# Moving the first feed-forward gate into its norm, reordering the feed-forward pools, and starting the last stage's weights before its norm

## The chip, the cores and the metric

The kernel runs on one core of a Trainium2 chip. The core has five engines, each with its own instruction queue that it works off strictly in order: TensorE (PE, matrix products; its weight loads are shown as PEld), VectorE (DVE), ScalarE (ACT), GpSimd (POOL) and SyncE (SP), which here only issues DMA transfers. The engines wait for each other by semaphores. The metric is the device time of one execution in microseconds (us).

## The reference

Two layers work on 256 context and 256 latent tokens of width 1024. All data are float32.

```python
for layer in range(2):
    # six modulation vectors for each of the two segments, from the conditioning vector
    sh1, sc1, g1, sh2, sc2, g2 = split(silu(c) @ mod_w[layer] + mod_b[layer], 6)
    h = rmsnorm(x, norm_mix_g) * (1 + sc1) + sh1
    x = x + g1 * mixer(h)              # layer 0: GLA and mLSTM heads; layer 1: SSD scan
    h = rmsnorm(x, norm_ffn_g) * (1 + sc2) + sh2
    u = depthwise_conv(h @ w_up)       # 1024 -> 2 * 2816
    x = x + g2 * ((silu(u_g) * u_a) @ w_down)
return rmsnorm(x_latent, final_norm_g) # layer 1 only needs the latent tokens after its mixer
```

## The kernel before

Activations are kept transposed: eight tiles `xT[k]` of 128 channels by 512 tokens. A float32 product is made of three matrix products of rounded parts (`mm3`, L186 to L188): high weights by high activations (`wh`, `hh`), low weights by high activations (`wl`, `hh`), high weights by low activations (`wh`, `hl`). Weights come through a `Stream`: a 1 MB load into a `raw` tile (L159; the very first one in two halves, L159 and L167), whose two halves ("units" of eight 128x128 blocks) are split by `split`: ACT writes `wh` (L174), then POOL or DVE writes `wl` (L175). The streams of the feed-forward up projections give all of L175 to POOL. A stream starts its next load as soon as one of its two `raw` buffers is free.

`Norm` gathers squares on ACT (L294), sums them over channels with matrix products against ones (`colsum`, L132), takes a reciprocal root in a row of short DVE steps (`rsqrt`, L112 to L123), and spreads the result over partitions (`spread`, L140, copied by ACT, L141). `norm_mod` then makes, for each of eight k: a DVE product (L323), ACT's `hh` (L329) and DVE's `hl` (L331). Layer 0 does this for two segments, so 16 steps of each kind; layer 1's last stage for one, so 8.

The modulation vectors come in chunks, twelve a layer. A chunk loads 2 MB of `modw` (L241, tiles `rawm`), runs eight 32-row matrix products (L249; the trace counts each twice), and `mod_out` copies the result by ACT (L269), transposes it on PE (L272) and reduces it on DVE (L276, L277). Chunks 10 and 11 of a layer are the feed-forward gate, g2. Most chunks of layer 1 are "fills": a stream calls one of them with each of its loads.

Three places matter here.

**Place one** is the end of layer 0's mixer, from 290 us to 355 us. The program there writes four head ends (`finish`: DVE and ACT steps, and transposes L739), with layer 0's chunks 10 and 11 among them, loaded into the mixer's buffers `b4`. Then the out-projection follows, 192 matrix products of 128x512.

**Place two** is layer 0's feed-forward norm and the first up product behind it, from 355 us. PE fills the norm with chunk (1,2). The first product works on four output tiles at once, k by k, which makes 96 matrix products of 128x512.

**Place three** is the last stage, from 1010 us: the end of layer 1's out-projection (`odd_out`), whose weights `wout` come by DMA; its norm; and the first up product (`project(0)`, 48 matrix products of 128x256). Between `odd_out`'s fourth and fifth output tile the program loads both gate chunks of layer 1, 4 MB. After `project(0)`, PE works through 22 rounds of up and down products, and POOL splits the weights for nearly all of them.

The order of instructions on each engine is the program's order, but for what the scheduler of the language moves by priorities. A buffer pool opened later may lie on memory that an earlier pool has just given up; its first writes then wait for the last readers of what lay there.

## Time and profile before

| what | value |
|---|---|
| runs | 1277.53, 1278.04, 1280.91 us (median 1278.04) |
| the profiled execution's own time | 1280.36 us |
| its span (first to last instruction) | 1278.6 us |
| PE busy | 1227.3 us, 96% of the span, at a mean granted clock of 0.989 |
| DVE busy | 928.4 us, 73% |
| ACT busy | 593.9 us, 46% |
| POOL busy | 424.4 us, 33% |
| DMA | 191.45 MB, 150 GB/s on average |

PE is busy nearly throughout, so the time is the work of PE, plus the places where PE waits, plus what it loses where its clock is at half. All three places of the change are among those.

### The profile page before, as it was taken

How to read it: one execution, taken by the hardware profiler on the slowest of the kernel's cores; microseconds unless marked ns; L12 is line 12 of the kernel's file. 1: busy time of each engine (PE TensorE's matmuls, PEld its weight loads, DVE VectorE, ACT ScalarE, POOL GpSimd, SP SyncE). 2: the span in 40 equal slices, each digit the busy share in tenths (PEclk: the TensorE clock that was granted, in tenths of full speed). 3: DMA queues.
4: the chain of work that ended last, by engine and by line, in shares of the span. 5: the costliest groups of instructions: out<-in, count | busy, mean ns of one | idle time of the engine just before them, and what ended most of it. 6: DMA issues, size and time to landing. Idle time of an engine off the chain costs nothing. (4 is left out here: it accounts for less than half of the span.)

```text
span 1278.6 us, 18743 instructions
## 1 busy us (share of the span) xinstructions
PE 1227.3 (96%) x7094; PEld 1001.2 (78%) x7094; DVE 928.4 (73%) x2064; ACT 593.9 (46%) x937; POOL 424.4 (33%) x246
## 2 busy tenths in 40 slices
PE   7989999999999999999999999999999998999996
PEld 5557787876867767888888897888887886999994
DVE  5483889487567776227776478888888955999997
ACT  4463345344344443214443246665656554655552
POOL 0100000000125555326666000022222314899992
PEclk9989999999999999999999999999999998999998
DMA  9556202334436565232211224453544394455431
GB/s 372 211 178 231 105 27 72 136 107 165 165 110 269 220 232 191 74 129 99 99 66 59 90 92 122 163 157 118 175 130 136 99 345 150 165 197 175 178 114 64
DMA packets 40107, 191.45 MB, mean 150 GB/s; under 512 B 4609, under 2 KB 10569, under 8 KB 21073
## 3 DMA queue, kind: packets, MB, share of 16 engines
q1 hardware_dynamic: 36512, 185.48, 41.6%
q10 hardware_dynamic: 3504, 4.77, 1.2%
q8 instruction: 56, 0.92, 0.3%
q14 instruction: 35, 0.28, 0.1%
HBM read 189.03 MB, written 1.20 MB: 149 GB/s over the span
## 5 line engine op out<-in xcount | busy, mean ns | idle before, releaser
L175 POOL TENSOR_TENSOR wl<-raw,wh 128x1024 fp32r<-128x1024 f32 x120 | 289.3, 2418 | 494.3 <-ACT wh L174 492.3
L174 ACT ACTIVATE wh<-raw 128x1024 fp32r<-128x1024 f32 x226 | 237.1, 1054 | 154.3 <-PE gps L188 98.2
L186 PE MATMUL gps<-hh,wh 128*128 128x512 f32 (+1 forms) x824 | 291.1, 354 | 6.9 <-ACT hh L329 4.9
L187 PE MATMUL gps<-hh,wl 128*128 128x512 f32 (+1 forms) x824 | 290.0, 352 | 1.1 <-DVE wl L175 1.1
L188 PE MATMUL gps<-hl,wh 128*128 128x512 f32 (+1 forms) x824 | 290.1, 353 | 0.0
L800 DVE SCALAR_TENSOR_TENSOR y<-mps,fcw,y 128x255 f32<-128x255 f32 (+3 forms) x592 | 245.5, 432 | 47.0 <-ACT y L794 33.5
L186 PEld LDWEIGHTS gps<-hh,wh 128*128 128x128 f32 x824 | 155.7, 189 | 42.9 <-issue 12.5
L175 DVE TENSOR_TENSOR wl<-raw,wh 128x1024 fp32r<-128x1024 f32 x106 | 129.8, 1234 | 78.0 <-ACT wh L174 77.9
L188 PE MATMUL mps<-hl,wh 128*128 128x256 f32 (+1 forms) x544 | 174.8, 322 | 1.4 <-DVE hl L331 1.4
L186 PE MATMUL mps<-hh,wh 128*128 128x256 f32 (+1 forms) x544 | 175.6, 323 | 0.3 <-ACT hh L329 0.3
L187 PE MATMUL mps<-hh,wl 128*128 128x256 f32 (+1 forms) x544 | 175.0, 322 | 0.0
L187 PEld LDWEIGHTS gps<-hh,wl 128*128 128x128 f32 x824 | 156.1, 189 | 24.0 <-issue 3.2
L188 PEld LDWEIGHTS gps<-hl,wh 128*128 128x128 f32 x824 | 156.1, 190 | 20.9 <-issue 1.7
L186 PEld LDWEIGHTS mps<-hh,wh 128*128 128x128 f32 x544 | 103.7, 191 | 15.5 <-issue 7.0
L188 PEld LDWEIGHTS mps<-hl,wh 128*128 128x128 f32 x544 | 103.5, 190 | 9.1 <-DVE hl L331 1.6
L187 PEld LDWEIGHTS mps<-hh,wl 128*128 128x128 f32 x544 | 103.6, 190 | 7.8
L800 DVE SCALAR_TENSOR_TENSOR y<-gps,fcw,y 128x189 f32<-128x189 f32 (+3 forms) x180 | 77.5, 438 | 22.0 <-ACT y L794 18.2
L794 ACT ACTIVATE y<-mps,fcw 128x256 f32<-128x256 f32 (+1 forms) x68 | 41.1, 638 | 89.0 <-PE mps L188 89.0
L186 PE MATMUL gps<-mh,wh 128*128 128x512 f32 (+1 forms) x198 | 73.5, 371 | 0.0
L188 PE MATMUL gps<-ml,wh 128*128 128x512 f32 (+1 forms) x198 | 73.5, 371 | 0.0
L187 PE MATMUL gps<-mh,wl 128*128 128x512 f32 (+1 forms) x198 | 73.4, 371 | 0.0
L342 DVE SCALAR_TENSOR_TENSOR x<-gps,mod,x 128x256 f32<-128x256 f32 x56 | 24.2, 478 | 45.1 <-PE gps L188 45.1
(293 smaller groups left out, 1899.5 us busy)
## 6 DMA issues: line engine op xcount, KB each, us to landing
raw<-in_up SPq DMA_DIRECT2D x42, 1024.0 KB, 4.9
rawm<-in_modw SPq DMA_DIRECT2D x36, 1024.0 KB, 6.7
raw<-in_win SPq DMA_DIRECT2D x32, 1024.0 KB, 5.3
raw<-in_dn SPq DMA_DIRECT2D x20, 1024.0 KB, 5.6
raw<-in_wout SPq DMA_DIRECT2D x10, 1024.0 KB, 6.2
rawm<-in_mods SPq DMA_DIRECT2D x8, 1024.0 KB, 14.2
R<-crd SPq DMA_DIRECT2D x32, 256.0 KB, 4.2
rawm<-in_modw SPq DMA_DIRECT2D x8, 512.0 KB, 6.3
```

Of the source, the lines that this page charges most:

```text
L174: s.activation(out=hi[:, :n], in_=rw, func=AF.Copy)
L175: self.eng(u).tensor_tensor(out=lo[:, :n], in0=rw, in1=hi[:, :n].bitcast(F32), op=ALU.subtract)
L186: te.matmul(out=ps, lhsT=lhi, rhs=rhi, start=first, stop=False)
L187: te.matmul(out=ps, lhsT=llo, rhs=rhi, start=False, stop=False)
L188: te.matmul(out=ps, lhsT=lhi, rhs=rlo, start=False, stop=last)
L342: v.scalar_tensor_tensor(out=xT[m][:, a:b], in0=ps[:, a - base:b - base], scalar=gt[:, m, ci:ci + 1], in1=xT[m][:, a:b], op0=ALU.mult, op1 ...
L794: self.E.s.activation(out=y, in_=ps, func=AF.Identity, scale=self.fcw[:, c + 4:c + 5], bias=self.fcw[:, c + 9:c + 10])
L800: self.E.v.scalar_tensor_tensor(out=o, in0=i, scalar=self.fcw[:, ti * 10 + wi:ti * 10 + wi + 1], in1=o, op0=ALU.mult, op1=ALU.add)
```

## The change

First, layer 0's chunks 10 and 11 no longer stand among the head ends. Their loads are issued after the last `finish`, chunk 10 into `b4`, chunk 11 into the mixer's `tok` buffers. Their matrix products are written after the out-projection, so they lie in the norm; chunk 11's `mod_out` is called after `norm_mod` (`rest()`). Chunk (1,2), which lay in the norm, becomes the first of the fills.

Second, the feed-forward's pools are opened in another order: `fw` (a table of convolution weights) and `ur` first, then `fp` and `fs`. `ur` holds the raw weights of the up projection in both layers; in the last stage the down projection, which used `ur` before, uses the general pool.

Third, in the last stage `early` splits the first two up units and loads only chunk (1,10) between output tiles; chunk (1,11) is loaded behind `odd_out`. Chunk (1,10)'s matrix products lie in the norm now. `issue_after` holds back, in the scheduler's order, chunk 10's output until the last step of `rsqrt`, and chunk 11's output and the convolution's first steps until the last `hh` of the norm.

```diff
     with ExitStack() as st:
-        even_mixer(E, st, acts, pss0, nrm.add)
+        rest = even_mixer(E, st, acts, pss0, nrm.add)
...
     r = nrm.row()
-    mod_chunk(1, 2, rawp, mps)
     acts = norm_mod(0, 3, 4, SEGS, r)
+    rest()
...
-    E.mod_chunk(0, 10, sp, E.vps, "b4", 4, 4)
     finish(0)
     finish(1)
     finish(2)
-    E.mod_chunk(0, 11, sp, E.vps, "b4", 4, 4)
     finish(3)
+
+    mods = [list(E.mod_load(0, 10, sp, "b4", 4, 4)), []]
+    for i in range(2):
+        raw = T_([P, 4, 516], "tok", bufs=2).rearrange("p a b -> p (a b)")[:, :2048]
+        nc.sync.dma_start(out=raw, in_=A["modw"][0, 11, :, i * 2048:(i + 1) * 2048])
+        mods[1].append(raw)
...
+    E.mod_go(0, 10, mods[0], E.gps)()
+    return E.mod_go(0, 11, mods[1], E.gps)
...
+        fw, self.ur = st.enter_context(E.tc.tile_pool(name="fw", bufs=1)), st.enter_context(E.tc.tile_pool(name="ur", bufs=2))
+        self.fcw = fw.tile([P, NFC], F32, tag="fcw", name=E.nm("fcw"))
+        E.nc.scalar.dma_start(out=self.fcw, in_=E.A["fcw"][l])
         self.fp = st.enter_context(E.tc.tile_pool(name="fp", bufs=1))
         self.fs = st.enter_context(E.tc.tile_pool(name="fs", bufs=6))
...
-    up = E.Stream(A["up1"], 44 * KD, ahead=2, eng=lambda u: g)
-    dn = E.Stream(A["dn1"], FF * KD, pool=ur, eng=lambda u: g if u < FF - 2 else v, parts=lambda u: dw if u < FF - LAG else E.wp)
+    up = E.Stream(A["up1"], 44 * KD, ahead=2, pool=ur, eng=lambda u: g, parts=lambda u: dw if u < 2 else E.wp)
+    dn = E.Stream(A["dn1"], FF * KD, eng=lambda u: g if u < FF - 2 else v, parts=lambda u: dw if u < FF - LAG else E.wp)
...
-    odd_out(E, gated, nrm.add, lambda: mods.extend((list(E.mod_load(1, 10, ur)), list(E.mod_load(1, 11, mw)))))
+
+    def early():
+        up.split(0)
+        up.split(1)
+        mods.append(list(E.mod_load(1, 10, mw)))
+
+    odd_out(E, gated, nrm.add, early)
+    mods.append(list(E.mod_load(1, 11)))
+
     turn(0)
     turn(4)
-    E.mod_go(1, 10, mods[0], mps)
     r = nrm.row()
-    E.mod_go(1, 11, mods[1], mps)
+    gate10 = E.mod_go(1, 10, mods[0], mps)
+    with tc.issue_after(E.last["rsqrt"]):
+        gate10()
+    gate11 = E.mod_go(1, 11, mods[1], mps)
     acts = E.norm_mod(1, 3, 4, SEGS[1:], r)
+    normed = E.last["norm"]
+    with tc.issue_after(normed):
+        gate11()
```

On PE, at place two (the norm between the out-projection and the first up product), this stood before; `rawm` is chunk (1,2):

```order
L132 MATMUL vps_3008<-ones,acc 128x128 x4
L249 MATMUL mps_3042<-rawm_3043,spad 32x512
L132 MATMUL vps_3008<-ones,t_558_3006 128x128 x4
L249 MATMUL mps_3042<-rawm_3043,spad 32x512 x3
L249 MATMUL mps_3042<-rawm_3049,spad 32x512 x4
L272 MATMUL mps_3057<-c_104,t_569_3055 128x128 x3
L140 MATMUL vps_3036<-c_104,ry_3024 128x128 x4
L272 MATMUL mps_3057<-c_104,t_569_3055 128x128
L186 MATMUL gps_3148<-hh_3068,wh_3154 128x512
L187 MATMUL gps_3148<-hh_3068,wl_3155 128x512
```

and this stands now (line numbers are 2 higher); `gps_2980` is chunk 10, `tok` chunk 11, `vps_3223` chunk (1,2):

```order
L134 MATMUL vps_2968<-ones,acc 128x128 x4
L251 MATMUL gps_2980<-rawm_2678,spad 32x512
L134 MATMUL vps_2968<-ones,t_550_2966 128x128 x4
...
L251 MATMUL gps_2980<-rawm_2684,spad 32x512 x2
L274 MATMUL gps_2991<-c_104,t_554_2989 128x128 x4
L251 MATMUL gps_2998<-tok_2686,spad 32x512 x4
L251 MATMUL gps_2998<-tok_2688,spad 32x512 x4
L142 MATMUL vps_3023<-c_104,ry_3011 128x128 x4
L251 MATMUL vps_3223<-rawm_3224,spad 32x512 x4
L251 MATMUL vps_3223<-rawm_3230,spad 32x512 x4
L188 MATMUL mps_3125<-hh_3032,wh_3130 128x512
```

Chunk 10 takes the place that chunk (1,2) had, chunk 11 stands ahead of the spread (L140, now L142), and chunk (1,2) behind it. The transposes of chunks 11 and (1,2) stand in the middle of the first up product. The first load of the up projection is written to memory where the `tok` buffers lie, so it waits for PE's products from `tok`.

On ACT, at place three (from the last square of the norm to the first convolution steps), this stood before; `t_1611` is chunk 10, `t_1619` chunk 11:

```order
L174 ACTIVATE wh_9690<-raw_9660 128x1024
L294 ACTIVATE t_1603_9507<-x_95 128x256
L908 COPY xt<-mps_9529 128x512
L908 COPY xt<-mps_9535 128x512
L269 COPY t_1611_9550<-mps_9541 128x512
L141 COPY rstd_9559<-vps_9573 128x256
L269 COPY t_1619_9586<-mps_9577 128x512
L141 COPY gate<-vps_10862 128x512
L329 ACTIVATE hh_9597<-t_1621_9595,mod_3_115 128x256
```

and this stands now; `t_1619` is chunk 10, `t_1646` chunk 11:

```order
L296 ACTIVATE t_1604_9517<-x_95 128x256
L917 COPY xt<-mps_9543 128x512
L917 COPY xt<-mps_9549 128x512
L271 COPY t_1619_9582<-mps_9573 128x512
L143 COPY rstd_9555<-vps_9569 128x256
L331 ACTIVATE hh_9602<-t_1622_9600,mod_3_115 128x256
...
L331 ACTIVATE hh_9644<-t_1643_9642,mod_3_115 128x256
L271 COPY t_1646_9648<-mps_9591 128x512
L176 ACTIVATE wh_9665<-raw_9663 128x1024
```

Two weight splits that stood just ahead of the last square, and the two copies between `rstd` and the first `hh`, are gone from there; chunk 11's copy comes after all eight `hh`. On PE, chunk 11's transposes still stand ahead of `project(0)`'s first product:

```order
L142 MATMUL vps_9569<-c_104,ry_9557 128x128 x2
L274 MATMUL mps_9584<-c_104,t_1619_9582 128x128 x4
L251 MATMUL mps_9591<-rawm_9527,spad 32x512 x4
L251 MATMUL mps_9591<-rawm_9529,spad 32x512 x4
L142 MATMUL vps_10865<-c_104,mod_5_117 128x128 x4
L274 MATMUL mps_9650<-c_104,t_1646_9648 128x128 x4
L188 MATMUL mps_9661<-hh_9602,wh_9261 128x256
```

Both chunks' products now lie in this norm, where before only chunk 11's did.

## Rows read from the trace of the kernel before

**Rows 1.** The page: busy time, share of the span and instructions of each engine.

```profile
PE 1227.3 (96%) x7094; PEld 1001.2 (78%) x7094; DVE 928.4 (73%) x2064; ACT 593.9 (46%) x937; POOL 424.4 (33%) x246
```

**Rows 2.** Timeline of PE, 295 to 316 us: start, length, what, idle time before.

```profile
300.69 1.05 PE L249 MATMUL vps<-rawm,spad 128*32 128x512 f32 x4
304.43 1.05 PE L249 MATMUL vps<-rawm,spad 128*32 128x512 f32 x4 [2.69 <-DMA rawm<-in_modw]
305.41 0.50 PE L188 MATMUL gps<-hl,wh 128*128 128x512 f32 x1
...
307.67 1.06 PE L249 MATMUL vps<-rawm,spad 128*32 128x512 f32 x8
308.67 0.50 PE L186 MATMUL gps<-hh,wh 128*128 128x512 f32 x1
...
314.78 0.60 PE L272 MATMUL vps<-c,t 128*128 128x128 f32 x4
315.13 0.48 PE L186 MATMUL gps<-hh,wh 128*128 128x512 f32 x1
```

**Rows 3.** Timeline of PE, 354 to 375 us.

```profile
355.14 1.05 PE L132 MATMUL vps<-ones,acc 128*128 128x128 f32 x8
...
358.19 1.92 PE L249 MATMUL mps<-rawm,spad 128*32 128x512 f32 x14
...
361.24 0.60 PE L140 MATMUL vps<-c,ry 128*128 128x128 f32 x4
...
363.97 0.60 PE L186 MATMUL gps<-hh,wh 128*128 128x512 f32 x1 [2.02 <-ACT hh L329]
```

**Rows 4.** Windows: length, busy PE, PEld, DVE, ACT, POOL, clock, DMA share, GB/s.

```profile
362.00:364.00 2.00, 0.03 (x1) 0.03 (x1) 1.93 (x7) 1.45 (x4) 0.00 (x0) 1.00 1.03 430
364.00:366.00 2.00, 2.00 (x5) 1.61 (x6) 2.00 (x6) 1.04 (x3) 0.00 (x0) 0.55 1.00 422
366.00:368.00 2.00, 2.00 (x7) 1.57 (x6) 2.00 (x6) 1.31 (x3) 0.00 (x0) 0.59 0.94 397
1030.00:1042.00 12.00, 11.41 (x98) 10.68 (x97) 5.19 (x11) 2.97 (x7) 0.00 (x0) 1.00 1.02 423
```

**Rows 5.** Timeline of SP, 285 to 400 us: the first load of the up projection.

```profile
322.54 0.33 SPq L159 DMA_DIRECT2D raw<-in_up  x1
```

**Rows 6.** The page: two groups of instructions, and one kind of DMA issue.

```profile
L175 POOL TENSOR_TENSOR wl<-raw,wh 128x1024 fp32r<-128x1024 f32 x120 | 289.3, 2418 | 494.3 <-ACT wh L174 492.3
L174 ACT ACTIVATE wh<-raw 128x1024 fp32r<-128x1024 f32 x226 | 237.1, 1054 | 154.3 <-PE gps L188 98.2
...
raw<-in_up SPq DMA_DIRECT2D x42, 1024.0 KB, 4.9
```

**Rows 7.** Timelines of DVE and of POOL, 336 to 376 us.

```profile
369.63 0.47 DVE L331 SCALAR_TENSOR_TENSOR hl<-t,mod,hh 128x256 fp32r<-128x256 f32 x1
...
372.86 3.13 DVE L331 SCALAR_TENSOR_TENSOR hl<-t,mod,hh 128x256 fp32r<-128x256 f32 x3 [1.57 <-ACT hh L329]
...
372.51 2.41 POOL L175 TENSOR_TENSOR wl<-raw,wh 128x1024 fp32r<-128x1024 f32 x1 [13.62 <-ACT wh L174]
```

**Rows 8.** The chain that ended last, 1000 to 1110 us.

```profile
1029.19 13.30 DMA raw<-in_wout
...
1063.62 1.04 ACT wh L174
...
1066.21 2.28 DVE rw L113
```

**Rows 9.** Timelines of PE, then of POOL, 1030 to 1085 us.

```profile
1062.18 0.61 PE L132 MATMUL vps<-ones,acc 128*128 128x128 f32 x4
...
1076.03 0.39 PE L186 MATMUL mps<-hh,wh 128*128 128x256 f32 x1 [0.30 <-ACT hh L329]
...
1083.47 0.39 PE L188 MATMUL mps<-hl,wh 128*128 128x256 f32 x1 [1.42 <-DVE hl L331]
...
1063.79 4.66 POOL L175 TENSOR_TENSOR wl<-raw,wh 128x1024 fp32r<-128x1024 f32 x2 [3.47 <-ACT wh L174]
```

More of the change, by code (lines that the diff above doesn't have):

```diff
@@ L106, in block_kernel @@
     g.memset(ones, 1.0)
+    last = {}
     def rsqrt(ss, scale, eps):
@@ L122, in rsqrt @@
         v.scalar_tensor_tensor(out=w, in0=w, scalar=-0.5, in1=m, op0=ALU.mult, op1=ALU.mult)
-        v.scalar_tensor_tensor(out=y, in0=w, scalar=1.5, in1=y, op0=ALU.add, op1=ALU.mult)
+        last["rsqrt"] = v.scalar_tensor_tensor(out=y, in0=w, scalar=1.5, in1=y, op0=ALU.add, op1=ALU.mult).ins
         return y
@@ L250, in mod_go @@
                 k += 1
-        mod_out(l, 4 * j, 4, ps, psa)
+        return lambda: mod_out(l, 4 * j, 4, ps, psa)
     def mod_chunk(l, j, pool=rawp, psa=vps, tag="raw", n=2, bufs=None):
-        mod_go(l, j, mod_load(l, j, pool, tag, n, bufs), psa)
+        mod_go(l, j, mod_load(l, j, pool, tag, n, bufs), psa)()
     def mod_part(q, pool, psa):
@@ L328, in norm_mod @@
             for ci, a, b in segs:
-                s.activation(out=h_[:, a:b], in_=y[:, a:b], func=AF.Identity, bias=sh[:, k, ci:ci + 1])
+                last["norm"] = s.activation(out=h_[:, a:b], in_=y[:, a:b], func=AF.Identity, bias=sh[:, k, ci:ci + 1]).ins
             for ci, a, b in segs:
@@ L386, in block_kernel @@
     fill0 = [lambda j=j: mod_chunk(0, j) for j in (4, 5, 8, 9, 6, 7)]
-    fill1 = [lambda j=j: mod_chunk(1, j) for j in (3, 0, 1, 4, 5, 8, 9, 6, 7)]
+    fill1 = [lambda j=j: mod_chunk(1, j) for j in (2, 3, 0, 1, 4, 5, 8, 9, 6, 7)]
     E.fill0, E.W0 = fill0, W0
@@ L785, in __init__ @@
         self.E, self.n, self.lo = E, n, n - TL
+        fw, self.ur = st.enter_context(E.tc.tile_pool(name="fw", bufs=1)), st.enter_context(E.tc.tile_pool(name="ur", bufs=2))
+        self.fcw = fw.tile([P, NFC], F32, tag="fcw", name=E.nm("fcw"))
+        E.nc.scalar.dma_start(out=self.fcw, in_=E.A["fcw"][l])
         self.fp = st.enter_context(E.tc.tile_pool(name="fp", bufs=1))
         self.fs = st.enter_context(E.tc.tile_pool(name="fs", bufs=6))
-        self.fcw = self.fp.tile([P, NFC], F32, tag="fcw", name=E.nm("fcw"))
-        E.nc.scalar.dma_start(out=self.fcw, in_=E.A["fcw"][l])
     def centre(self, ps, ti):
@@ L793, in centre @@
         c = ti * 10
-        self.E.s.activation(out=y, in_=ps, func=AF.Identity, scale=self.fcw[:, c + 4:c + 5], bias=self.fcw[:, c + 9:c + 10])
+        self.last = self.E.s.activation(out=y, in_=ps, func=AF.Identity, scale=self.fcw[:, c + 4:c + 5], bias=self.fcw[:, c + 9:c + 10]).ins
         return y, ps, ti
@@ L831, in conv_ffn @@
     cv = Conv(E, st, 0, T)
-    ur = st.enter_context(E.tc.tile_pool(name="ur", bufs=2))
-    up = E.Stream(E.A["up0"], 44 * KD, fill, 1, 2, pool=ur, eng=lambda u: g)
+    up = E.Stream(E.A["up0"], 44 * KD, fill, 1, 2, pool=cv.ur, eng=lambda u: g)
     first = []
@@ L890, in last_ffn @@
     cv = Conv(E, st, 1, TL)
-    ur, dw, mw = (st.enter_context(tc.tile_pool(name=n, bufs=2)) for n in ("ur", "dw", "mw"))
+    ur = cv.ur
+    dw, mw = (st.enter_context(tc.tile_pool(name=n, bufs=2)) for n in ("dw", "mw"))
     lp = st.enter_context(tc.tile_pool(name="lp", bufs=1))
     LAG = 4
-    up = E.Stream(A["up1"], 44 * KD, ahead=2, eng=lambda u: g)
-    dn = E.Stream(A["dn1"], FF * KD, pool=ur, eng=lambda u: g if u < FF - 2 else v, parts=lambda u: dw if u < FF - LAG else E.wp)
+    up = E.Stream(A["up1"], 44 * KD, ahead=2, pool=ur, eng=lambda u: g, parts=lambda u: dw if u < 2 else E.wp)
+    dn = E.Stream(A["dn1"], FF * KD, eng=lambda u: g if u < FF - 2 else v, parts=lambda u: dw if u < FF - LAG else E.wp)
     fng = lp.tile([P, D], F32, tag="fng", name="fngr")
@@ L935, in project @@
             pa = E.gemm_f(up, 16 * j + 8, KD, acts, 256, T, lambda: both[:, TL:])
-        return cv.centre(pg, FF + j), cv.centre(pa, j)
+        r = cv.centre(pg, FF + j), cv.centre(pa, j)
+        centred[:] = [cv.last]
+        return r
     hm = []
@@ L953, in last_ffn @@
     part = lambda: None
-    nxt = project(0)
+    with tc.issue_after(normed):
+        nxt = project(0)
     for j in range(FF):
@@ L961, in last_ffn @@
         if j in more:
-            more[j]()
+            with tc.issue_after(centred[0]):
+                more[j]()
         h, part = cv.tile(cg, ca, v, part, "", LAG + 2, v if j == FF - 1 else g)
```

1 line of the change is left out of this document (added).

## The prediction

> **What bounds the kernel now.** I read first the page's busy times: PE is busy in 96% of the span [rows 1], so time is won or lost only where PE waits or where its clock is at half. The list of PE's waits and the timelines of the engines at the three places then show where that is. Place one: PE waits 2.69 us for a chunk of modulation weights, with the chunk's matrix products around it [rows 2]. Place two: from the norm's first sum at 355.14 to the first up product at 363.97 lie 8.8 us, of which PE spends the last 2.02 waiting for `hh` [rows 3]; after it the granted clock is 0.55 and 0.59 in two windows of 2 us, between the levels 1.2 and 2.4 GHz, which costs 2 x 0.45 + 2 x 0.41 = 1.7 us [rows 4]. Place three: the chain that ended last runs through a `wout` load of 13.30 us [rows 8], while DMA moves 423 GB/s [rows 4], about as much as in any window I saw; then through a weight split and a DVE step of 2.28 us [rows 8]; from the first sum at 1062.18 to the last wait of `project(0)` at 1083.47 [rows 9], and to its end some 0.5 us later, it is 21.8 us.
>
> **Place one, gain 9.4 us.** The products and the transposes of chunks 10 and 11 leave. From 300.69 to 305.41 that is 4.7 us with the wait in it; 1.0 us from 307.67 to 308.67, and there are four such rows in all, at 296.80, 307.67, 310.49 and 312.33: 4.0 us; the transposes take 0.35 (314.78 to 315.13), twice: 0.7 [rows 2]. Sum 9.4. What stood in line around them on ACT (two copies) and DVE goes too, so I let no new wait of PE for the head ends come up; if the 2.69 us also covered that chain, up to 2.7 us of the gain is gone. So the out-projection ends, and the norm's sum begins, at 345.8 instead of 355.1.
>
> **Place two, loss 10.4 us.** Chunk 10 takes the place of chunk (1,2), same shape, same time. Chunk 11's 1.92 [rows 3] goes ahead of the spread, which moves from 6.1 to about 8.2 us behind the sum: 2.0 lost. Chunk (1,2) fills the wait for `hh` and costs nothing there. The `hh` would let the up product start at 345.8 + 8.8 + 2.0 = 356.6.
>
> But the weights are late. Before, the first up load was issued at 322.54 [rows 5], 41 us ahead. Now it writes where `tok` lay and waits for chunk 11's products, so for 353.9. A 1 MB load lands 4.9 us after its issue [rows 6]; half of it is less by 0.5 MB at 430 GB/s [rows 4], so I estimate 3.7 (bounds 3 and 4.9). Then ACT takes 1.05 and POOL 2.42 [rows 6]: 353.9 + 3.7 + 1.1 + 2.4 = 361.1 for the first low products, 4.5 behind `hh`. This is 2.9 earlier than 363.97. The clock's 1.7 us stays, since PE again stands idle before; the transposes of chunks 11 and (1,2) now lie inside the product: 0.7.
>
> Then there is the company that POOL's splits now have. Before, the four splits of the first product were done by 359, before DVE's norm steps began. Now they run beside them. An `hl` step takes 0.47 us alone, so three take some 1.2; three of them took 3.13 where a POOL split of 2.41 ran from 372.51 [rows 7]: about 1.9 lost to one split. ACT's order makes a chain of it: the second, third and fourth `wh` stand behind the `hh` steps of the next k, which wait for DVE, which waits for POOL's split before. A link is 2.4 (split) + some 1.3 (three or four DVE steps) + 1.1 (`wh`), 4.8 us. So the weights of k = 2 come at 365.9, of k = 4 at 370.7. PE now runs two output tiles through k = 0 to 5 first: 36 products at 0.2265, 8.2 us, and 1.7 for the clock would end at 371.0; chained, the last DVE step for k = 5 ends some 2 us after 370.7, and PE at about 374.1. So 3.2 lost (bounds: 0, if DVE's steps slip in between, and 9.7, four whole splits). Net of places one and two: 2.9 - 0.7 - 3.2 = **1.0 us slower**.
>
> The Trainium skill, page "SBUF — State Buffer", section "Who interferes with whom", says that a VectorE instruction with two SBUF inputs contends with a GpSimd instruction that reads SBUF, and that the one which comes second blocks wholly; the row of 3.13 us agrees. By it alone the four splits could cost DVE 9.7 us, and with my other terms the two places would lose 7.5.
>
> **Place three, gain 4.0 us.** Ahead of the `wout` load that ends the wait of 13.30 stand 4 MB of chunks; now 3 MB (two chunk loads, two halves and one whole of up weights). With DMA at 423 GB/s [rows 4] 1 MB is 2.4 us, so I let `odd_out` end 2.4 earlier (bounds 0, if the load is held by a buffer, and 3.6, if the 16 products of chunk 10, which leave here, count too). In the norm, the last square no longer stands behind the split at 1063.62 and the one before it: 1.7 us; the reciprocal root no longer stands beside POOL's splits from 1063.79 [rows 9], so its step takes 0.17 as its neighbours do instead of 2.28 [rows 8]: 2.1. But `project(0)` does not start early. Its first product stands behind chunk 11's transposes, whose copy on ACT now comes after all eight `hh`. From the sum at 1062.18: square and second sum 1.7, root 2.4, spread and copy 1.0, 16 DVE steps of 0.4 with the last `hh` 0.8 before their end, so `hh` at 1073.5; copy 0.6, transposes 0.6, so the first product at 1074.7 instead of 1076.03 [rows 9]; 48 products of 0.119, 5.7, and again 1.8 for the clock after 4.8 us of idleness: 1082.2 instead of 1083.9. So 1.7, not 3.8. Sum with 2.4: 4.1, say **4.0 us faster**.
>
> All else counts as nothing: the table of convolution weights waits on ACT's queue for chunk 11 too, but ahead of the spread's copy, which is later anyway; ten fills instead of nine move the same products; the reordered pools give no new wait that I find behind the first load. In the last stage POOL has four splits (9.7 us) more to do after the norm than before. Behind the copy at 1074.1 ACT makes `wh`, and the third up unit's split ends at 1077.6; six more at 2.42 (two of them for the down product) and the seventh unit's ends at 1092.1. PE wants it four units of 24 x 0.119 = 2.85 behind 1082.2, at 1093.6: 1.5 us to spare.
>
> **The sum.** 1.0 slower and 4.0 faster: 3.0 us. Against the profiled execution's own 1280.36 this is 1277.4; that execution was 2.3 above the median, so against 1278.04 it is **1275.0 us**. This measurement can tell about 0.3%, 3.8 us, from no change; 3.0 lies inside.
>
> **The rivals.**
> *The splits and DVE don't hurt, or only little.* For it: DVE has gaps of a step's length while POOL waits for ACT. Against it: the row of 3.13 us. Then places one and two gain 2.2, and with an earlier landing 3; total 6.2 to 7: 1271.5. Chance 0.22.
> *The weights aren't late at all,* because the load gets its memory or the product starts on its high parts. Then the first product starts at 356.6, without the clock's loss perhaps: 9.4 - 2.0 - 0.7 + 4.0 = 10.7: 1267.3. The order of reads and writes speaks against it. Chance 0.08.
> *`wout` lands no earlier,* since the new up loads cost as much or a buffer holds it: 0.6 gained, 1277.4, also no change that can be told. Chance 0.2.
> *Slower: POOL's splits in the norm block DVE one by one.* If each of the four costs PE its whole 2.42 us, the loss S is 9.7 instead of 3.2, and the total is 6.2 - S = -3.5; it tells as slower from S = 10.0, or from 7.6 if `wout` also stays where it was. What speaks for it is the same row, what speaks against it is that PE needs a new pair of weights only every 2.7 us and has slack at low clock. 1282.0. Chance 0.13. The page named above, read strictly, leads here.
>
> **How the numbers follow.** The forecast has 0.37, `wout` unmoved 0.2, both within 0.3%; with some of their tails outside, same 0.5. Faster is 0.22 + 0.08 and a tail of 0.06: 0.36. Slower is 0.13 and a small tail: 0.14. From 1270 (quick weights and no stalls, wholly) to 1281.5 (just short of the slower rival) no more than 2 in 10 is left out; the forecast's own range is 1273 to 1278.
>
> **What would show it.** Right: no wait of PE for `rawm` near 300 us; the norm's sum at about 346; the first up load issued at about 354 and the first low product at about 361; `hl` steps of 2 to 3 us beside POOL's splits; a wait for the third pair of weights; in the last stage the first norm sum near 1060 on the old clock, a root without a step of 2 us, a wait of some 5 us for ACT's copy of chunk 11 ahead of `project(0)`, and no wait of PE for `wl` behind it. Wrong: a first up load before 350; the norm sum later than 348; PE waiting for POOL's `wl` after 1085.

## The result, and the profile after

The changed kernel takes **1287.59 us** (median of 4 runs, 1285.82 to 1289.32), the kernel before beside it 1278.15 (4 runs): a ratio of 1.0065, with a 95% interval of 1.0043 to 1.0088. It is slower by 5.5 to 11.2 us; 1275.0 was forecast, with 1281.5 as the upper end. The profiled execution after has an own time of 1285.82 us, a span of 1284.0 and a mean granted clock of 0.986.

The page, busy time of each engine; [rows 1] before:

```profile
PE 1224.8 (95%) x7094; PEld 1003.9 (78%) x7094; DVE 925.2 (72%) x2064; ACT 594.0 (46%) x937; POOL 428.9 (33%) x246
```

PE is busy with as many instructions for 2.5 us less, and the span is 5.4 longer: the time that was added is mostly waits. Read between marks that the timelines of both have, the two kernels compare like this (us):

| stretch | before | after | difference |
|---|---|---|---|
| start to the first sum of place two's norm | 355.14 | 345.58 | -9.56 |
| that sum to the start of the 96th up product | 34.65 | 47.59 | +12.94 |
| to the first norm sum of layer 1 | 354.53 | 359.26 | +4.73 |
| to the end of layer 1's scan | 272.97 | 273.20 | +0.23 |
| to the first sum of place three's norm | 44.89 | 42.46 | -2.43 |
| to PE's last product | 204.60 | 204.21 | -0.39 |

They add up to +5.5, as the two executions differ (1285.82 - 1280.36). The medians differ by 9.4. Part of that is the stretch ahead of place two, which varies by some 3 us between executions: the sum stood at 355.1, 356.0 and 355.8 in three kernels with the old mixer's end, and at 345.6, 348.4, 348.7, 348.7 and 348.3 in five with the changed one (this profile and experiments 3, 4, 6 and 8). The gain ahead of place two is 9.6 in this pair and about 7.5 by the middle values.

Part of it is lost before place one. The first half of chunk 11 is loaded into `tok` long before the last `finish`, here at 244.73 (SP's timeline). It runs beside small loads of the mixer, and DVE waits for one of them (DVE's timeline):

```profile
244.73 0.33 SPq L773 DMA_DIRECT2D tok<-in_modw  x1
```

```profile
252.03 0.35 DVE L702 SCALAR_TENSOR_TENSOR b<-b,RQT,c_trineg 128x128 f32<-128x128 f32 x1 [2.63 <-DMA b<-prd]
```

PE's wait for DVE behind it (L662, near 254 us) is 2.1 to 2.8 us in all six kernels that load a chunk into `tok` (these five and experiment 5), and at most 0.9 in the five that do not.

Place two on PE, 340 to 380 us, where [rows 3] stood:

```profile
345.58 1.05 PE L134 MATMUL vps<-ones,acc 128*128 128x128 f32 x8
...
359.65 0.73 PE L188 MATMUL mps<-hh,wh 128*128 128x512 f32 x2 [2.67 <-ACT wh L176]
362.15 0.79 PE L189 MATMUL mps<-hh,wl 128*128 128x512 f32 x1 [1.76 <-POOL wl L177]
...
374.67 0.79 PE L189 MATMUL mps<-hh,wl 128*128 128x512 f32 x1 [4.42 <-POOL wl L177]
```

The wait for `hh` is replaced by three for weights, and the third, 4.42 us, is the largest of the kernel. Behind it the clock is at half a second time (windows; columns as in [rows 4]):

```profile
374.00:376.00 2.00, 1.33 (x3) 1.14 (x4) 0.90 (x1) 0.00 (x0) 2.00 (x2) 0.64 0.00 0
376.00:378.00 2.00, 2.00 (x6) 1.52 (x6) 0.00 (x0) 0.00 (x0) 1.14 (x1) 0.51 0.00 0
```

That is another 2 x 0.36 + 2 x 0.49 = 1.7 us. The first fall of the clock costs more than before, too:

```profile
362.00:364.00 2.00, 1.85 (x4) 1.49 (x5) 2.00 (x2) 0.00 (x0) 2.00 (x2) 0.50 0.93 393
364.00:366.00 2.00, 2.00 (x6) 1.59 (x5) 2.00 (x5) 0.51 (x1) 0.61 (x1) 0.50 0.30 57
366.00:368.00 2.00, 2.00 (x6) 1.56 (x6) 2.00 (x7) 1.89 (x4) 0.00 (x0) 0.57 0.88 336
```

From 362.15 to 367.80 PE makes 13 products, which at 0.2265 us each are 2.9 us; 2.7 are lost, where the kernel before lost 1.7. SP's timeline has the first up load, which [rows 5] had at 322.54:

```profile
353.87 0.33 SPq L161 DMA_DIRECT2D raw<-in_up  x1
```

ACT's first split of it (ACT's timeline) shows that this half landed 4.7 us after its issue:

```profile
358.55 1.06 ACT L176 ACTIVATE wh<-raw 128x1024 fp32r<-128x1024 f32 x1 [1.68 <-DMA raw<-in_up]
```

POOL's timeline has the four splits of the first product, as two pairs ([rows 7] before):

```profile
359.74 4.87 POOL L177 TENSOR_TENSOR wl<-raw,wh 128x1024 fp32r<-128x1024 f32 x2 [309.75 <-DMA raw<-in_up]
368.04 9.10 POOL L177 TENSOR_TENSOR wl<-raw,wh 128x1024 fp32r<-128x1024 f32 x2 [3.44 <-ACT wh L176]
```

The first pair takes 4.87 us, two splits of 2.4; the second 9.10, although the data of its first split were there. DVE's timeline in the same time shows the company:

```profile
360.04 2.33 DVE L333 SCALAR_TENSOR_TENSOR hl<-t,mod,hh 128x256 fp32r<-128x256 f32 x1 [1.34 <-ACT hh L331]
362.29 2.59 DVE L325 SCALAR_TENSOR_TENSOR t<-x,mod,rstd 128x256 f32<-128x256 f32 x1
364.81 0.87 DVE L333 SCALAR_TENSOR_TENSOR hl<-t,mod,hh 128x256 fp32r<-128x256 f32 x2
...
367.98 1.27 DVE L325 SCALAR_TENSOR_TENSOR t<-x,mod,rstd 128x256 f32<-128x256 f32 x3
...
371.94 0.48 DVE L325 SCALAR_TENSOR_TENSOR t<-x,mod,rstd 128x256 f32<-128x256 f32 x1
372.33 2.56 DVE L333 SCALAR_TENSOR_TENSOR hl<-t,mod,hh 128x256 fp32r<-128x256 f32 x1
```

Beside the first pair two DVE steps are held, for 2.33 and 2.59. Beside the second pair it is the other way round: from 364.81 to 372.33 DVE's steps follow each other every 0.4 us, and only from 372.3 on does a step show the hold of a running split. 372.3 and one split of 2.4 make 374.7, where PE goes on. So POOL stood still from 368.04 to 372.3. The step at 372.33 is the last of the run and not behind it. By the order of the steps it needs the `hh` that ACT ends at 372.25, just ahead of it:

```profile
371.75 0.51 ACT L331 ACTIVATE hh<-t,mod 128x256 fp32r<-128x256 f32 x1
```

Place three, PE's timeline ([rows 9] before), then DVE's step that took 2.28 in [rows 8], then the end of `project(0)` on ACT, then POOL:

```profile
1068.09 0.61 PE L134 MATMUL vps<-ones,acc 128*128 128x128 f32 x4
...
1080.12 1.11 PE L274 MATMUL mps<-c,t 128*128 128x128 f32 x4 [4.38 <-ACT t L271]
```

```profile
1070.42 0.17 DVE L115 TENSOR_SCALAR rw<-rm 128x2 int32<-128x2 int32 x1
```

```profile
1088.16 1.02 ACT L803 ACTIVATE y<-mps,fcw 128x256 f32<-128x256 f32 x2 [1.41 <-PE mps L190]
```

```profile
1081.11 16.59 POOL L177 TENSOR_TENSOR wl<-raw,wh 128x1024 fp32r<-128x1024 f32 x7 [33.20 <-ACT wh L176]
```

From the sum to the end of `project(0)` it is 20.1 us (before, 1083.9 - 1062.18 = 21.7). The wait for ACT's copy of chunk 11 and the quick root are there.

### The profile page after: what moved, and what is told of

Same layout as the page of the kernel before. It is cut to its first block, busy times and chain, and to the rows that moved or that the text cites. A ratio compares the mean times of both kernels' runs of the same rounds, so it can differ in the third digit from the quotient of the medians.

```text
span 1284.0 us, 18750 instructions
## 1 busy us (share of the span) xinstructions
PE 1224.8 (95%) x7094; PEld 1003.9 (78%) x7094; DVE 925.2 (72%) x2064; ACT 594.0 (46%) x937; POOL 428.9 (33%) x246
## 5 line engine op out<-in xcount | busy, mean ns | idle before, releaser
L177 POOL TENSOR_TENSOR wl<-raw,wh 128x1024 fp32r<-128x1024 f32 x120 | 293.6, 2457 | 485.9 <-DMA raw<-in_up 309.7
L188 PEld LDWEIGHTS gps<-hh,wh 128*128 128x128 f32 x824 | 155.5, 189 | 38.8 <-issue 10.9
L189 PE MATMUL mps<-hh,wl 128*128 128x256 f32 (+1 forms) x544 | 177.7, 327 | 6.2 <-POOL wl L177 6.2
```

What stands on the lines that cost most here:

```text
L177: self.eng(u).tensor_tensor(out=lo[:, :n], in0=rw, in1=hi[:, :n].bitcast(F32), op=ALU.subtract)
L188: te.matmul(out=ps, lhsT=lhi, rhs=rhi, start=first, stop=False)
L189: te.matmul(out=ps, lhsT=llo, rhs=rhi, start=False, stop=False)
```

## Experiments

**1. The last stage alone, and 2. with the reordered pools.** The first takes the changed kernel and gives layer 0 back its mixer's end and its pool order; the second gives back only the mixer's end. The core of both edits:

```diff
-        rest = even_mixer(E, st, acts, pss0, nrm.add)
+        even_mixer(E, st, acts, pss0, nrm.add)
...
+    mod_chunk(1, 2, rawp, mps)
     acts = norm_mod(0, 3, 4, SEGS, r)
-    rest()
...
+    E.mod_chunk(0, 10, sp, E.vps, "b4", 4, 4)
     finish(0)
     finish(1)
     finish(2)
+    E.mod_chunk(0, 11, sp, E.vps, "b4", 4, 4)
     finish(3)
```

> Only the last stage's part of the change; layer 0 (mixer, chunks, pool order) as before. Theory A (all of the loss lies in layer 0's norm and first up product, where the weights are late and POOL's splits and DVE's norm steps hold each other up): layer 0's 8.1 to 8.3 us of loss vanish and the last stage's gain of 2.9 us stays, so about 1275.3 us against 1278.2 before. Rival B (the last stage gives nothing, its gain in the profile is chance): 1278. Rival C (the loss comes from the last stage's or the pools' new waits in other places): 1283 or more.

> The last stage's part and the reordered pools in both layers, but layer 0's gate chunks among the head ends and chunk (1,2) in the norm as before. Theory A: the order of the pools alone costs nothing, since no chunk lies in the tok buffers then and the first up load is issued well before the norm: within 1 us of the run with the last stage alone, about 1275. Rival C (the place of the raw weights in memory makes the first load late by itself): first up load after 340 us, 1280 or more.

Measured: 1278.22 us (10 runs) and 1278.42 (10 runs) against 1278.33, ratios 0.999 [0.9973, 1.0007] and 1.0002 [0.9984, 1.002]. Neither can be told from no change. So the loss is not in the last stage nor in the pool order, but in layer 0's mixer and norm. In the first one's profile the stretch from the scan's end to PE's last product is 3.6 us shorter than before (245.9 and 249.5), of the size that was forecast; the runs allow 3.4 faster to 0.9 slower.

**3. The first four splits on DVE.** The pair is then DVE's own, and POOL has nothing to do in the norm.

```diff
-    up = E.Stream(E.A["up0"], 44 * KD, fill, 1, 2, pool=cv.ur, eng=lambda u: g)
+    up = E.Stream(E.A["up0"], 44 * KD, fill, 1, 2, pool=cv.ur, eng=lambda u: v if u < 4 else g)
```

> The changed kernel, with the first four splits of layer 0's up weights on DVE instead of POOL. Theory A (beyond the late load, POOL's split and DVE's norm steps block each other): PE's waits of 1.8 and 4.4 us for wl shrink, the first up product ends at about 388 instead of 393 us, and the time falls by some 4 to 5 us, to about 1283, although DVE has four steps of 1.2 us more. Rival D (only the late load matters): the product still ends at 392 or later, 1286 to 1288.

Measured: 1287.93 us, 1.0071 [1.0052, 1.0089], as the changed kernel. DVE wrote its four low parts only behind nearly all norm steps (from 371.50 on). PE waited as long at another place, for a chunk's transposes, which here stand ahead of the first low product:

```profile
371.07 1.12 PE L274 MATMUL gps<-c,t 128*128 128x128 f32 x4 [7.46 <-ACT t L271]
```

This doesn't tell contention from mere lateness; it is inconclusive.

**4. Chunk 11 behind `project(0)`.** Its output is called after the first up product of the last stage.

```diff
-    with tc.issue_after(normed):
-        gate11()
...
         nxt = project(0)
+        gate11()
```

> The changed kernel, with chunk 11's output of the last stage written behind the first up product instead of ahead of it. Theory A (PE idles 4.4 us before that product only because chunk 11's transposes stand ahead of it and their copy behind all hh): the product starts at about 1075 instead of 1080.9 and ends 5 us earlier, of which POOL, whose splits begin no earlier than 1081, may take back some: 1283 to 1285. Rival E (POOL bounds the stage, so an earlier start of PE is given back as waits for wl): 1287, with waits of PE for wl of 4 us or more behind the product.

Measured: 1290.88 us, 1.0098 [1.0068, 1.0128]: no gain; the interval overlaps that of the changed kernel. In its profile `project(0)` ends 14.9 us behind the norm's sum instead of 20.1, but the first down product stands 44.9 behind it instead of 43.5. Between them PE waits for DVE, ACT and POOL by turns, 3.6 us behind `project(0)`, half of it here (PE's timeline):

```profile
1109.73 0.36 PE L188 MATMUL mps<-hh,wh 128*128 128x256 f32 x1 [1.83 <-DVE y L809]
```

Only 0.6 of it is for POOL, so rival E's waits of 4 us and more for `wl` did not come. In both kernels POOL has seven splits in a row behind the norm. That these make the stage as late as before is not shown.

**5. Late weights with the old order.** As experiment 2, with chunk (1,2) loaded into the mixer's `tok` tiles, so that the first up load waits for its products. The norm and the four-tile order stay as before.

```diff
-        even_mixer(E, st, acts, pss0, nrm.add)
+        c12 = even_mixer(E, st, acts, pss0, nrm.add)
...
-    mod_chunk(1, 2, rawp, mps)
+    mod_go(1, 2, c12, mps)()
```

> Layer 0's gate chunks among the head ends and chunk (1,2) in the norm, as before; but chunk (1,2) is loaded into the tok buffers, so that the first up load waits for its products. The last stage as in the changed kernel. Only the late load is added here. Theory A (late weights, and then POOL's splits and DVE's norm steps in each other's way, make the loss): load issued at about 360 us, first low product at about 368, waits for wl of 4 us and more, first up product about 11 us later than before; 1286 to 1289 us. Rival F (the loss comes from the moved chunks themselves, the late load is worth its 4 us at most): 1279 to 1282.

Measured: 1285.54 us (10 runs), 1.0051 [1.0035, 1.0067]; of this some 5 us arise earlier (the norm's sum stands at 360.8): the load into `tok` stands in the mixer's way as in the changed kernel, and PE's wait at L662 is 2.80. So the time says little here, and the stretch has to: from the norm's sum to the 96th product it is 37.9 us, against 34.7 before. Late weights alone cost 3.2, between the 11 of theory A and the nothing of rival F. POOL's splits and the first DVE step behind a pause:

```profile
371.25 9.02 POOL L177 TENSOR_TENSOR wl<-raw,wh 128x1024 fp32r<-128x1024 f32 x3 [319.49 <-DMA raw<-in_up]
```

```profile
373.58 1.93 DVE L333 SCALAR_TENSOR_TENSOR hl<-t,mod,hh 128x256 fp32r<-128x256 f32 x1 [0.56 <-ACT hh L331]
```

Three splits are 7.2 us; they took 1.8 longer. 371.25 + 1.8 = 373.0, which is where DVE's run of steps (from 368.18) breaks for 0.56 us.

**6. Early weights with the new order.** The raw weights of the first up projection lie in the general pool, which is free early; all else is the changed kernel.

```diff
-    up = E.Stream(E.A["up0"], 44 * KD, fill, 1, 2, pool=cv.ur, eng=lambda u: g)
+    up = E.Stream(E.A["up0"], 44 * KD, fill, 1, 2, eng=lambda u: g)
```

> The changed kernel, with layer 0's raw up weights in the general pool (two buffers, shared with the fills) instead of ur, so that the first load does not wait for chunk 11. Theory A: first load at about 340 us or before, first low product at about 357 instead of 362, no waits for wl in the first product, its end before 384 instead of at 393. Behind it the two shared buffers may make the fills and the up loads wait for each other, which takes back an unknown part: 1277 to 1284 us in all. Rival F: the first product still ends at 390 or later.

Measured: 1306.03 us, 1.0225 [1.02, 1.025], because the fills now share two buffers with the weights and PE waits for them later (waits from 400 to 760 us):

```profile
PE vps L251 <- DMA rawm<-in_modw: 20.4, 8, 5.7
```

The place in question is still readable. All splits are done by 352.4, the first product stands 10.9 us behind the sum (14.1 in the changed kernel), PE waits for no `wl` and its granted clock stays at 1.00 from 358 to 386 us; the 96th product is 36.5 behind the sum, though three chunks lie in between. With early weights the two-tile order costs little: at a clock of 1.00 throughout, as in experiment 9, the four-tile order with two chunks took 33.1, to which a third chunk adds some 2.3.

**7. Both gate chunks as fills.** Layer 0's chunks 10 and 11 leave the mixer as in the changed kernel, but go to the head of the up projection's fills; layer 0's norm and pools are as before, the last stage is the changed one.

```diff
-    fill1 = [lambda j=j: mod_chunk(1, j) for j in (2, 3, 0, 1, 4, 5, 8, 9, 6, 7)]
+    fill1 = [lambda l=l, j=j: mod_chunk(l, j) for l, j in ((0, 10), (0, 11), (1, 3), (1, 0), (1, 1), (1, 4), (1, 5), (1, 8), (1, 9), (1, 6), (1, 7))]
```

> A version meant to keep the gain and avoid the loss: layer 0's gate chunks become the first two fills of the up stream (their result is wanted only at the end of that feed-forward), pools of layer 0 in the order of before, last stage as in the changed kernel. Theory A: the mixer ends some 9 us earlier, the norm and the first up product are as before, and two more chunks in the stream cost 2.4 us each: 4.6 us gained in layer 0, and 0 to 2.9 in the last stage: 1271 to 1274 against 1278.3. Rival G (PE's time off the mixer is only lent, and the fills' waits take it back): 1277 to 1279.

Measured: **1275.67 us** (12 runs) against 1279.08, 0.9963 [0.9945, 0.9981]. PE's timeline:

```profile
345.64 1.05 PE L134 MATMUL vps<-ones,acc 128*128 128x128 f32 x8
...
354.47 0.58 PE L188 MATMUL gps<-hh,wh 128*128 128x512 f32 x1 [2.03 <-ACT hh L331]
```

The norm is the old one (8.8 us to the first product, 34.7 to the 96th), at the new, early time. The stretch behind the 96th product is 361.1 us instead of 354.5, with two chunks more in it: a chunk as a fill costs 3.3 us.

**8. Chunk 11's output later, hence the four-tile order.** The changed kernel, with `rest` called by the first fill instead of ahead of the first product. PE's timeline shows four tiles at once as before; the late load stays. Why the order hangs on this call is not shown. That the banks of PSUM are handed out in another order is likely, but chunk 11's products stand in the norm in both, and so its first bank is held in both.

```diff
-    rest()
+    fill1[0] = lambda: (mod_chunk(1, 2), rest())
```

> The changed kernel, but chunk 11's output (its ACT copy, transposes and DVE steps) is called with the first fill, inside the first up product, instead of ahead of it. PE then runs the product over four output tiles per k, as before the change, and not over two tiles through k = 0 to 5; the first up load is as late as in the changed kernel. Theory H (late weights and the two-tile order together make the loss: two tiles want new weights every 1.4 us per k, four every 2.7, which hides the slow splits): from the norm's sum to the last of the 96 products about 40 us instead of 47.6, no wait of 4 us for wl, 1279 to 1281 in all. Theory A without the order (the late load and the contention alone): 46 us or more, 1286 to 1288.

Measured: 1281.83 us (10 runs), 1.0032 [1.0018, 1.0047], that is 5.8 us less than the changed kernel. PE's waits from 335 to 395 us, and POOL's timeline:

```profile
PE gps L188 <- ACT wh L176: 3.1, 1, 3.1
PE gps L189 <- POOL wl L177: 1.3, 1, 1.3
```

```profile
371.25 14.10 POOL L177 TENSOR_TENSOR wl<-raw,wh 128x1024 fp32r<-128x1024 f32 x4 [3.44 <-ACT wh L176]
```

The load is as late as in the changed kernel (8.3 us behind the sum in both), and POOL stands still as long: four splits are 9.7 us and took 14.1, so 4.4 are lost. But PE doesn't wait for them, since in this order it wants the third pair of weights only behind 48 products, some 0.3 us after they are there. From the sum to the 96th product it is 41.2 us instead of 47.6.

**9. Fills, with the last stage as before.** The kernel before, with chunks 10 and 11 as fills as in experiment 7, and nothing else.

```diff
-    E.mod_chunk(0, 10, sp, E.vps, "b4", 4, 4)
     finish(0)
     finish(1)
     finish(2)
-    E.mod_chunk(0, 11, sp, E.vps, "b4", 4, 4)
     finish(3)
```

> The kernel before, changed only in that layer 0's gate chunks become the first two fills; its last stage is that of before. Tells whether the gain of the version with fills comes from layer 0 or from the last stage. If from layer 0 alone (theory A: 9 us off the mixer less 4.8 in the stream): 1274 to 1276, ratio near that of the version with the new last stage. If the last stage carries it: 1278 to 1279.

Measured: **1274.61 us** (12 runs) against 1278.95, 0.9973 [0.996, 0.9987]. So the gain of experiment 7 comes from layer 0 alone; the changed last stage adds nothing that these runs can tell.

Experiments 5 to 8 make a square, though not all with the same number of chunks (us from the norm's sum to the 96th product, one profile each; a chunk more is 1.9 of products and 0.4 of transposes):

| weights | order | kernel | chunks in it | us | waits for `wl` |
|---|---|---|---|---|---|
| early | four tiles | before, and 7 | 2 | 34.7 | none |
| late | four tiles | 5 | 2 | 37.9 | 2.9 |
| late | four tiles | 8 | 3 | 41.2 | 1.3 |
| early | two tiles | 6 | 3 | 36.5 | none |
| late | two tiles | changed | 3 | 47.6 | 1.8 and 4.4 |

The profiles differ by the clock, too: the first cell is 33.1 in experiment 9, where the clock stays at 1.00, and 35.8 in experiment 2, where it is at half for longer. So differences of 1 or 2 us tell nothing here. Late weights alone cost some 3 to 4 (37.9 and 34.7; 41.2, and 37.0 as an estimate from 34.7 and 2.3 for a third chunk). The largest part, 6.4, needs both: late weights, and an order that asks for them twice as fast. What was left is why POOL stood still. Five small kernels, which leave out the whole reference, measure that by itself: a run of DVE steps (128x256, two operands in SBUF, 0.40 us each) that ACT sets off, and two splits of POOL (128x1024) beside it.

**10. A split beside a run.** Runs of 16 and 32 steps, 32 steps with one operand, and four splits with eight steps.

```python
for i in range(32):
    v.scalar_tensor_tensor(out=lo[i % 4], in0=y, scalar=sc[:, 0:1], in1=x[:, 256:], op0=ALU.add, op1=ALU.subtract)
for i in range(2):
    g.tensor_tensor(out=wl[i], in0=raw[:, i * 1024:i * 1024 + 1024], in1=wh[i].bitcast(F32), op=ALU.subtract)
```

> This kernel leaves out all of the reference and measures only how POOL's splits (128x1024, two operands in SBUF) and DVE's steps (128x256) get on with each other: POOL alone; DVE alone; two splits that come about 1.5 to 2 us after the start of a run of 16 DVE steps with two operands in SBUF; the same with a run of 32; the same with 32 steps of one operand; four splits with eight DVE steps that come in the middle of them. Alone both theories expect 2.4 us for a split and 0.4 for a step in a run. Theory P (while DVE's steps of two operands follow each other without a gap, POOL's split can't begin): with the run of 16 (6.5 us) the first split ends about 2.4 us behind the run's end, some 7 us after its own start; with 32 (13 us) also 2.4 behind the run's end, some 13 us after its start, so the length of the wait follows the length of the run; the steps stay at 0.4. With one operand the split takes 2.4 and ends inside the run. In the last part DVE's first step is held until the end of the split that runs, some 1 to 2.4 us. Theory Q (the two share in turns, which is what my chain of 4.8 us a link took): the split ends inside either run, and takes 2.4 to 3.5 us, and single steps of the run take up to 2.4.

Measured: two splits took 4.66 us alone, 5.10 and 5.11 beside the runs of 16 and 32, and 4.84 beside one-operand steps. Two steps of each run of two-operand steps took 2.5 us. In the last part four splits took 10.01, and each held one step of DVE, for 2.5 us. The splits came 0.9 us into their runs, earlier than meant. Theory P fell, so far.

**11. The same without any wait inside a run** (`out=z`, a tile of its own for each step).

> Like the run before it, this kernel leaves out the whole reference. One thing differs: each DVE step writes a tile of its own, so that within a run no step waits for any semaphore (in the run before, each waited for an older step of its own engine, which was always done). Theory P2 (a split of POOL gets in only where DVE stops for a wait, however short, and a run without waits holds it): beside the run of 16 two-operand steps (6.4 us) the first split ends some 2.4 us behind the run's end, and beside the run of 32 (12.7 us) as well, so two splits take about 5 + 3.5 to 5 and 5 + 10 to 11.5 us, and no step is longer than 0.5. Theory Q2 (they share in turns whatever the waits): two splits take 5.1 again in both, and two steps 2.5 each. Both expect no hold with one operand (4.8 for two), and in the last part steps held for 2.5, one to a split.

Measured, POOL's timeline (the run of 16, of 32, and of 32 with one operand), then DVE's run of 16:

```profile
21.48 5.06 POOL L117 TENSOR_TENSOR wl<-raw,wh 128x1024 fp32r<-128x1024 f32 x2 [8.50 <-ACT wh L87]
33.51 5.06 POOL L127 TENSOR_TENSOR wl<-raw,wh 128x1024 fp32r<-128x1024 f32 x2 [6.96 <-ACT wh L87]
51.87 4.69 POOL L137 TENSOR_TENSOR wl<-raw,wh 128x1024 fp32r<-128x1024 f32 x2 [13.30 <-ACT wh L87]
```

```profile
20.19 10.59 DVE L115 SCALAR_TENSOR_TENSOR lo<-y,sc,x 128x256 f32<-128x256 f32 x16 [1.44 <-ACT y L81]
```

16 steps are 6.4 us; 10.59 says that 4.2 went to two splits, one step held for each. Waits were not it either.

**12. Traits of the norm.** Results in fp32r; ACT busy throughout; the norm's own chain of step, `hh` and step; changing operands.

> Again without the reference; four stretches, each with two splits of POOL (4.7 us alone) that come after the start of a run of DVE steps, and each with one thing that the norm in the changed kernel has and the two runs before had not: first, 32 steps whose result is fp32r; second, 32 steps with ACT at work beside them throughout; third, the norm's own chain of step, ACT's high part and step, sixteen times; fourth, 32 steps on changing operands of 512-wide tiles. The runs before showed splits of 2.5 us and one step of 2.5 us to a split, whatever the length of the run. In the changed kernel one split took 6.6, beside 11 steps of 0.4. Theory R (one of these four makes POOL wait for a pause of DVE): in that stretch the two splits take 7 to 15 us while DVE's steps stay at 0.4, in the others 5.1. Theory S (none of them; it is something else in that stretch of the kernel, so far unknown): 5.1 in all four.

Measured, POOL's timeline:

```profile
8.34 4.97 POOL L98 TENSOR_TENSOR wl<-raw,wh 128x1024 fp32r<-128x1024 f32 x2 [7.90 <-ACT wh L87]
27.00 5.08 POOL L98 TENSOR_TENSOR wl<-raw,wh 128x1024 fp32r<-128x1024 f32 x2 [13.70 <-ACT wh L87]
47.90 13.45 POOL L98 TENSOR_TENSOR wl<-raw,wh 128x1024 fp32r<-128x1024 f32 x2 [15.82 <-ACT wh L140]
63.57 5.06 POOL L98 TENSOR_TENSOR wl<-raw,wh 128x1024 fp32r<-128x1024 f32 x2 [2.22 <-ACT wh L87]
```

The norm's chain does it: 13.45 us for two splits. DVE's timeline has the end of its run:

```profile
54.79 2.06 DVE L133 SCALAR_TENSOR_TENSOR nl<-nt,sc,nh 128x256 fp32r<-128x256 f32 x5
```

It ended at 56.8; 56.8 + 4.7 = 61.5, and 47.90 + 13.45 = 61.35. POOL waited for the end of the run.

**13. Which trait of the chain.**

> Without the reference, as the three runs before. The norm's own chain held two splits of POOL for 13.45 us, until DVE's run was over, and the other three stretches did not. Four stretches now, each with one trait of that chain: first, two kinds of operation in turn; second, one kind, with every second step waiting on a tile of ACT's that is ready; third, one kind, with ACT reading the result of every step; fourth, one kind, two scalar columns in turn. The trait that matters shows 11 to 14 us for its two splits, the others 5.1. Theory K: it is the kind of operation in turn (first), since there alone DVE's next step differs from the one before. Theory W: it is the semaphores to and from ACT (second or third). If all four stay at 5.1, it takes several together, and the mechanism stays open.

Measured: 4.97, 12.64, 5.09 and 5.06 us. It is the second stretch, with waits on ACT. But there the splits also came later in the run, at 4.6 us instead of 1.0 to 1.3, as they had in the norm's chain (3.8).

**14. Waits or lateness.**

> Without the reference, as the four runs before. In the two stretches where DVE's run held POOL's splits to its end, two things went together: DVE's steps waited, every second one, on tiles of ACT's that were ready, and the splits came 3.8 and 4.6 us into the run; where they got in, they came 0.9 to 1.3 us into it. Four stretches of 32 steps take the two apart: first, no waits and the splits 4.6 us into the run; second, waits on ACT and the splits about 1.2 us into it; third, waits on older steps of DVE's own, splits late; fourth, no waits, two tiles as second operand in turn, splits late. Theory L (late splits are held, whatever the waits): first, third and fourth show 11 to 13 us for two splits, the second 5.1. Theory W (the waits on ACT's tiles hold them): only the second shows it, with 14 us or more; the others 5.1.

Measured, POOL's timeline, then DVE's first run:

```profile
11.62 12.93 POOL L98 TENSOR_TENSOR wl<-raw,wh 128x1024 fp32r<-128x1024 f32 x2 [11.19 <-ACT wh L107]
26.87 4.99 POOL L98 TENSOR_TENSOR wl<-raw,wh 128x1024 fp32r<-128x1024 f32 x2 [2.32 <-ACT wh L126]
48.49 12.63 POOL L98 TENSOR_TENSOR wl<-raw,wh 128x1024 fp32r<-128x1024 f32 x2 [16.63 <-ACT wh L107]
66.67 12.63 POOL L98 TENSOR_TENSOR wl<-raw,wh 128x1024 fp32r<-128x1024 f32 x2 [5.55 <-ACT wh L107]
```

```profile
7.31 12.75 DVE L115 SCALAR_TENSOR_TENSOR lo<-y,sc,x 128x256 f32<-128x256 f32 x32
```

Theory L holds. A split that comes 4.3 us or more into a run waits for the run's end (7.31 + 12.75 = 20.06, and 4.66 for the two splits make 24.7; they ended at 24.55), whatever the steps wait for, and DVE loses nothing: 32 steps in 12.75. A split that comes 1.4 us into the run gets in, and then DVE loses a step's time to each split.

The changed kernel fits: its third split came 3.2 us into a run (364.81 to 368.04) and was held; so were the first split of experiment 5 (368.18 to 371.25) and the third of experiment 8. The first pair came in a pause of DVE and got through. One thing differs from the small kernels: in the changed kernel and in experiment 8 the split got in just ahead of the run's last steps, and the next step then took 2.6 us. In both, the `hh` of that step ended less than 0.1 us ahead of it, so such a step may work as a pause; no run here tests that.

## Why the prediction was wrong

**Place one was right in its terms, and the 345.58 for a forecast of 345.8 is partly luck.** The wait for the chunk and its products are gone. But the load of chunk 11 into `tok`, which no term of the sum had, costs PE some 2 us ahead of place one, and in four other profiles of the same mixer the sum stands between 348.3 and 348.7, where the prediction's own sign of being wrong begins. By the middle values the gain is nearer 7.5 than 9.4.

**Place two failed**, at the step "So 3.2 lost" and at the fills, which the prediction counted as nothing ("ten fills instead of nine move the same products"). Forecast were 10.4 us of loss there; it is 12.94 + 4.73 = 17.7.
- The late load was right to 0.1 us (353.87). The first low product came at 362.15, forecast 361.1: 1.3 later against the sum. Of this 1.0 is the estimate of 3.7 us for the landing of half a load, which took 4.7.
- The company of splits and steps was seen, but with the wrong one as the loser. The prediction let POOL's splits delay DVE in a chain of 4.8 us a link. The second pair of weights came even earlier than the 365.9 of that chain (364.61). The third came at 374.67 instead of 370.7, since DVE kept POOL out for 4.3 us: by experiments 12 to 14 that is what a run of DVE steps does to a split that comes late in it. The wait of 4.42 and the second fall of the clock, 1.7, are 6.1 us; experiment 8, which takes away the order that makes PE wait, is 6.4 shorter here. Of the 6.1, 3.2 were in the sum, so 2.9 were missing. The first fall of the clock, forecast at 1.7, cost 2.7: 1.0 more.
- Chunk (1,3), the first fill of the kernel before, lay in the first product there. Now (1,2) is the first fill, and (1,3) stands behind the 96th product, where there are nine chunks instead of eight. Taken out of the first product it saves its 1.92 of products and 0.35 of transposes; the stretch with one chunk more is 4.73 longer. That is 2.4 more than forecast. PE waits 1.8 there for copies and sums of chunks, as it did not before; 3.3 is what a fill costs in experiment 7.

Together 1.3 + 2.9 + 1.0 + 2.4 = 7.6, where 7.3 are missing. The share of the fills is read from the profiles and was not tested by itself.

**Place three was right in its terms, and smaller in sum.** `wout` brought 2.43 (forecast 2.4), the norm up to the end of `project(0)` 1.6 (forecast 1.7), and the root, the wait of 4.38 and the first sum (forecast near 1060 on the old clock; the scan ends 8.34 later in this profile, and 1068.09 - 8.34 = 1059.75) are as described. The 1.6 are still there at the first down product (43.5 us behind the sum, 45.1 before), but only 0.4 are left at PE's last product. One wait of 0.6 for DVE's convolution steps stands in between; where the rest goes is not shown. Measured alone, place three is not to be told from no change.

**The rivals.** The slower rival had the sign, but its loss of 9.7 from the splits is more than the 6.1 to 6.4 that were found, and its mechanism, POOL blocking DVE one by one, is not what cost the time. So where it came near, it was by luck. What the prediction held against it, that PE "has slack", is true only in the four-tile order. The range ended short of it.

The Trainium skill, page "SBUF — State Buffer", section "Who interferes with whom", says that the second of the two engines blocks wholly, and that issue order decides which it is. The runs agree: DVE's step is held for 2.5 us when a split is at work, and with one operand it is not held at all (two splits 4.69). The section speaks of one instruction that is waited for; here the runs differ: POOL waited for a whole run of them, 4.3 us in the kernel and 8 to 9 in experiments 12 to 14.

## What to carry to other kernels

Work that is moved off a waiting place has to go where PE streams anyway: the same two chunks as fills make the kernel 4 us faster, in the norm with borrowed buffers 9 us slower. When a change moves another product's output across a product's start, look at the order in which the product now asks for its weights before pricing anything late by the old order. A POOL split beside a gapless run of two-operand DVE steps should be ready before that run begins, or in one of its pauses. And a load that borrows a buffer can be issued far ahead of its place in the program: look at what small loads it runs beside.

## What was not expected of the hardware

A POOL split beside a run of two-operand DVE steps either gets in at once (it came 0.9 to 1.4 us into the run: 5.0 to 5.1 us for two, and DVE loses 2.1 us to each) or not before the run ends or comes to a step whose `hh` is only just ready (3.1 us or more into it: up to 8.8 us of standing still, in which DVE loses nothing). Between 1.4 and 3.1 us nothing was measured, and why the age of the run should matter stays open: the waits inside the run, its operations, its operands, the type of its results and ACT's work beside it are excluded by experiments 11 to 14, each in one run.
